# Split matmuls of a two-block transformer: first block sum of a weight tile formed as A22 plus A21 by a load and an adding DMA, and low parts of two tiles of the second FFN product by adding DMA

## The chip, the cores and the metric

The kernel runs on one core of one Trainium2 chip. The metric is the device time of one execution in microseconds (us). Before the change three runs took 1543.89, 1545.36 and 1546.64 us; the median is 1545.36 us.

## The reference

Two transformer blocks act on 256 latent tokens and 256 context tokens, with a model width of 1024. Each block has a feed-forward network (FFN), a mixer and a second FFN; the mixer of the first block is a gated short convolution, that of the second is attention with grouped keys. In the second block the context only feeds the attention, so the last FFN runs on the latent tokens alone. Every part sees a root-mean-square norm, a shift and a scale first and is added back through a gate:

```
def _modulate(t, g, shift, scale):
    return _rms(t, g) * (1 + scale) + shift
def _swiglu(h, w13, w2):
    gte, up = jnp.split(h @ w13, 2, axis=-1)
    return (jax.nn.silu(gte) * up) @ w2
lat = lat + 0.5 * mod[:, 0, 2] * _swiglu(_modulate(lat, norm_g[i, 0], mod[:, 0, 0], mod[:, 0, 1]), ffn_w13[i, 0], ffn_w2[i, 0])
```

FFN weights are 1024 x 5632 (`w13`) and 2816 x 1024 (`w2`), all in float32.

## The kernel before

**Split products.** TensorE (PE) gets each float32 operand as a high part (rounded to the type fp32r) and a low part (what is left), and one product is three matmuls: high x high (L136), low x high (L137), high x low (L138). ScalarE (ACT) copies a raw tile to its high part (L107, tiles `wh`), VectorE (DVE) subtracts to get the low part (L108, tiles `wl`); `split` does both. `split_far` (L111 to 114) does it without VectorE: ACT copies high (L112), ACT copies the negated high part into the low tile (L113), and a DMA issued by GpSimd (POOL) adds the raw weights from memory onto it (L114). Before the change only the block A22 of each weight tile goes this way (tiles `w4h`, `w4l`).

**Stages.** The FFNs with 512 tokens, (0,0), (0,1) and (1,0), run in thirds of 8, 7 and 7 column tiles of the 22. A third computes its column tiles of `h @ w13`, then `project` (L595) multiplies the gated result with the matching rows of `w2` for eight output tiles m = 0 to 7; `ws2` (L895) loads and splits the weights of output tile m. Tiles 0, 1 and 2 are asked for at the start of `project`, a further one whenever a tile is begun.

**Block products.** Most column tiles of `w13`, and those of the convolution's input product, are a `Pair` (L694): the weights of a tile are a 2 x 2 block matrix A11, A12, A21, A22, the activations a 2 x 2 block matrix B, and seven products of sums of blocks take the place of eight. The class `Blocks` holds the activation's blocks and their sums T1 to T4 (tiles `th`, `tl`); a `Pair` holds A11, A12, A22 and the sums S1 to S4. Its steps are `__init__` (loads, S1, and the splits of A11 and A12), `sums(0)` (S2 on VectorE, L732, and the split of the tile that holds S1 and S2), `sums(1)` (A22 by `split_far`, then S3 and S4 in one VectorE instruction, L740, and their split), and then the products on PE: `head` (A11, A12), `five` (S1), `six` (S2, S4), `seven` (S3), `four` (A22). In `__init__` SyncE (SP) loads r2 = [A22 | A12] (512 KB) and the right half of r1 = A11 (256 KB, L708); POOL writes -A22 into the left half of r1 (TENSOR_SCALAR, L710) and issues a DMA that adds A21 onto it (L713). So S1 = A21 - A22.

**Openings.** The convolution's product and the FFNs (0,1) and (1,0) begin with `opening` (L788): the last tiles of the stage before are still being finished while the norm of the first 256 tokens, then that of the other 256 tokens, is formed; two column tiles run without block products, half by half, and a `Pair` called `head` follows. `rms_sum` (L264) forms a norm: PE sums the squares (L269), ACT takes the root (L274), VectorE the reciprocal (L278), PE spreads it (L287), VectorE scales the activations (L299), and ACT and VectorE make the high and low parts (`bh` L391, `bl` L392, raw `hr` L396).

**Order of work.** A scheduler fixes the order of the instructions of each engine from the order of the code and from marks: what stands under `tc.issue_after(x)` comes behind the instruction x. Every engine then runs its list in order, and one that waits holds up all behind it. POOL's list holds L710, the adding DMAs L713 and L114, and the DMAs (L567) that add each gated result `yg` onto the residual `x`. Raw weights share 8 buffers (`wr`), the high and low tiles 4 each (`wh`, `wl`), A22's parts 2 each. L177 on VectorE are units of the modulation (scale, shift and gate of later stages) that fill gaps.

Of the kernel before, what the change touches and what calls it, by code (L numbers as in the profile page):

```python
# [9 lines left out]
F32 = mybir.dt.float32  # L10
# [3 lines left out]
ALU = mybir.AluOpType  # L14
AX = mybir.AxisListType

P = 128
# [3 lines left out]
T2 = 2 * S  # L21
# [27 lines left out]
def hybrid_kernel(ctx: ExitStack, tc: tile.TileContext, a: dict, out: bass.AP):  # L49
    nc = tc.nc  # L50
    const = ctx.enter_context(tc.tile_pool(name="const", bufs=1))
    wp = ctx.enter_context(tc.tile_pool(name="wp", bufs=2))
# [10 lines left out]
    def nm(s):  # L63
        uid[0] += 1
        return f"{s}{uid[0]}"
# [35 lines left out]
    def load_raw(src, n=1024):  # L101
        raw = wp.tile([P, 1024], F32, name=nm("wr"), tag="wr", bufs=8)
        nc.sync.dma_start(raw[:, :n], src)
        return raw

    def split(hi, lo, src):
        nc.scalar.activation(out=hi, in_=src, func=AF.Copy)  # L107
        return nc.vector.tensor_tensor(out=lo, in0=src, in1=hi.bitcast(F32), op=ALU.subtract)  # L108
# [139 lines left out]
        return get  # L248


    accs = {}

    def square_add(k, c0, c1):

# [9 lines left out]
    def rms_sum(s):  # L264

        pq = psmall("ss")
        for i in range(2):
            c = s * S + i * P
            nc.tensor.matmul(  # L269
                pq[:, S + i : S + i + 1], accs["t"][:, c : c + P], ones[:, 0:1],  # L270
                start=True, stop=True,
            )
        rs = tp.tile([P, 2], F32, name=nm("rs"), tag="rs")
        nc.scalar.activation(  # L274
            out=rs, in_=pq[:, S : S + 2], func=AF.Sqrt, scale=1.0 / D, bias=eps_t
        )
# [96 lines left out]
    class Blocks:  # L373
# [33 lines left out]
        def sums(self, n):  # L407

            r = self.raw
            b11, b12, b21, b22 = r[0, 0], r[0, 1], r[1, 0], r[1, 1]  # L410
            tt = nc.vector.tensor_tensor

            def keep(key, src):
                hi, lo = self.t[key] = hot("th"), hot("tl")
                split(hi, lo, src)

            if n == 0:
                tt(out=b11, in0=b12, in1=b11, op=ALU.subtract)
                keep("T1", b11)
            elif n == 1:  # L420
                tt(out=b12, in0=b22, in1=b12, op=ALU.add)
                tt(out=b22, in0=b22, in1=b11, op=ALU.add)
                keep("T2", b22)
            else:
                tt(out=b21, in0=b21, in1=b22, op=ALU.subtract)
                keep("T3", b12)
                keep("T4", b21)

    class FirstBlocks(Blocks):
# [13 lines left out]
        def sums(self):  # L443
            r = self.raw
            tt = nc.vector.tensor_tensor
            for key in ("T1", "T2", "T3", "T4"):
                self.t[key] = hot("th"), hot("tl")

            def keep(key, q, src):
                hi, lo = self.t[key]  # L450
                c = slice(q * T2, q * T2 + T2)
                split(hi[:, c], lo[:, c], src)

            b = lambda hf, s, q: r[2 * hf + q, s]
            for q in range(2):
                tt(out=b(0, 0, q), in0=b(0, 1, q), in1=b(0, 0, q), op=ALU.subtract)
                keep("T1", q, b(0, 0, q))
            for q in range(2):
                tt(out=b(0, 1, q), in0=b(1, 1, q), in1=b(0, 1, q), op=ALU.add)
                tt(out=b(1, 1, q), in0=b(1, 1, q), in1=b(0, 0, q), op=ALU.add)  # L460
# [236 lines left out]
    class Pair:  # L697
# [5 lines left out]

        def __init__(self, src, h):
            self.h, self.w, self.src = h, {}, src
            r2 = load_raw(src[:, 1024:2048])
            r1 = wp.tile([P, 1024], F32, name=nm("wr"), tag="wr", bufs=8)
            nc.sync.dma_start(r1[:, T2:], src[:, T2:1024])  # L708

            nc.gpsimd.tensor_scalar(  # L710
                out=r1[:, :T2], in0=r2[:, :T2], scalar1=-1.0, scalar2=None, op0=ALU.mult
            )
            nc.gpsimd.dma_start(out=r1[:, :T2], in_=src[:, :T2], accum_op=ALU.add)  # L713
            self.raw = [r1, r2]
            ts = half()
            for i, key in enumerate(("A11", "A12")):
                self.w[key] = [t[:, i * T2 : i * T2 + T2] for t in ts]
                split(*self.w[key], self.raw[i][:, T2:])

        def keep(self, keys, part):  # L720
            hi, lo = half()
# [4 lines left out]
        def sums(self, n):  # L726

            r1, r2 = self.raw
            s1, s2 = r1[:, :T2], r1[:, T2:]
            tt = nc.vector.tensor_tensor  # L730
            if n == 0:
                tt(out=s2, in0=s2, in1=s1, op=ALU.subtract)  # L732
                self.keep(("S1", "S2"), r1)
                return
            self.w["A22"] = [
                wp.tile([P, T2], F32R, name=nm(t), tag=t, bufs=2) for t in ("w4h", "w4l")
            ]
            split_far(*self.w["A22"], r2[:, :T2], self.src[:, 1024 : 1024 + T2])
            v = lambda t: t.rearrange("p (a c) -> p a c", a=2)
            tt(  # L740
                out=v(r2), in0=v(r2), in1=s2.unsqueeze(1).to_broadcast([P, 2, T2]),
                op=ALU.subtract,
            )
            self.keep(("S3", "S4"), r2)
# [44 lines left out]
    def opening(h, srcs, post):  # L789

        w = [load_w(srcs[0])]
        pp = [(psum("pg"), psum("pu")) for _ in range(2)]
        w13_mm(pp[0], w[0], h, range(KT), 0, S)
        flush(1)
        w.append(load_w(srcs[1]))
        at = w13_mm(pp[1], w[1], h, range(2), 0, S)
        with tc.issue_after(at):
            flush()
        with tc.issue_after(every[-1]):
            w13_mm(pp[1], w[1], h, range(2, KT), 0, S)  # L800
# [12 lines left out]

    def ffn(l, b, h, tot, gate, tail, gs=(), ev=(0, 0), z=None):
        gs = list(gs)
        i0 = 0
        for t, n in enumerate(THIRDS):
# [809 lines left out]
```

## Time and profile before

| | |
|---|---|
| median of 3 runs | 1545.36 us (1543.89 to 1546.64) |
| profiled execution | 1544.66 us |
| its span in the profile | 1542.9 us, so 1.8 us lie around it |
| PE busy | 1533.0 us, 99% |
| VectorE (DVE) busy | 1296.8 us, 84% |
| ACT busy | 850.5 us, 55% |
| POOL busy | 299.3 us, 19% |
| read from memory | 262.07 MB |

The profile shows one execution, with engine names as above; PEld is the weight load of a matmul, SP the queue of plain loads. A row of the timeline gives start and duration in us, engine, line, operation, output tile <- input tiles with their shape, and, in brackets, how long the engine was idle before and what ended that. Matmuls are pipelined: their durations overlap, and from start to start one with 256 columns takes 0.12 us and one with 512 columns 0.23 us. A larger distance from start to start is a stall of PE. A group of rows (`xN`) gives the total busy time and the mean in ns.

### The profile page before, as it was taken

How to read it: one execution, taken by the hardware profiler on the slowest of the kernel's cores; microseconds unless marked ns; L12 is line 12 of the kernel's file. 1: busy time of each engine (PE TensorE's matmuls, PEld its weight loads, DVE VectorE, ACT ScalarE, POOL GpSimd, SP SyncE). 2: the span in 40 equal slices, each digit the busy share in tenths (PEclk: the TensorE clock that was granted, in tenths of full speed). 3: DMA queues.
4: the chain of work that ended last, by engine and by line, in shares of the span. 5: the costliest groups of instructions: out<-in, count | busy, mean ns of one | idle time of the engine just before them, and what ended most of it. 6: DMA issues, size and time to landing. Idle time of an engine off the chain costs nothing.

```text
span 1542.9 us, 27460 instructions
## 1 busy us (share of the span) xinstructions
PE 1533.0 (99%) x10652; PEld 1424.7 (92%) x10652; DVE 1296.8 (84%) x1974; ACT 850.5 (55%) x1476; POOL 299.3 (19%) x265
## 2 busy tenths in 40 slices
PE   9999999999999999999999999999999999999999
PEld 7898998999999899989899899989999899998888
DVE  5889788898999999978979889958968788997676
ACT  5744554646665376446456476446456456774553
POOL 0003313402231012042142102142052002300000
PEclk9999999999999999999999999999999999999999
DMA  9568768775366645686796635786697743476562
GB/s 367 211 191 236 159 185 227 172 196 142 75 144 183 197 104 143 216 209 147 213 210 150 212 74 126 222 186 145 209 222 177 257 156 113 147 246 220 170 195 75
DMA packets 97474, 278.80 MB, mean 181 GB/s; under 512 B 11456, under 2 KB 13120, under 8 KB 97344
## 3 DMA queue, kind: packets, MB, share of 16 engines
q1 hardware_dynamic: 69408, 228.10, 45.8%
q0 software_dynamic: 25920, 47.20, 18.1%
q10 hardware_dynamic: 2016, 1.76, 0.4%
q8 instruction: 83, 1.36, 0.4%
q14 instruction: 47, 0.39, 0.1%
HBM read 262.07 MB, written 1.05 MB: 171 GB/s over the span
## 4 chain that ended last, share of the span: by engine, by line
PE 90%; DVE 5%; DMA 2%; issue 1%; ACT 1%; POOL 0%; SPq 0%; DVEq 0%; ACTq 0%; POOLq 0%
PE py L137 8%; PE py L136 8%; PE py L138 8%; PE p L138 8%; PE p L136 8%; PE p L137 8%; PE q L138 6%; PE q L136 6%; PE q L137 6%; PE py L144 2%; PE pu L144 2%; PE pg L144 2%; DMA wr<-in_w 2%; DVE wl L108 1%; PE py L146 1%
## 5 line engine op out<-in xcount | busy, mean ns | idle before, releaser
L107 ACT ACTIVATE wh<-wr 128x1024 fp32r<-128x1024 f32 (+2 forms) x454 | 401.3, 909 | 291.0 <-PE py L137 98.6
L108 DVE TENSOR_TENSOR wl<-wr,wh 128x1024 fp32r<-128x1024 f32 (+2 forms) x454 | 467.0, 1052 | 106.3 <-ACT wh L107 87.6
L177 DVE CUSTOM_DVE_ANT_0 junk<-wr,scbc,first 128x1024 bf16<-128x1024 f32 x209 | 271.0, 1296 | 2.3 <-DMA wr<-in_modT 0.3
L137 PE MATMUL py<-gl,wh 128*128 128x512 f32 (+1 forms) x570 | 213.4, 374 | 0.0
L136 PE MATMUL py<-gh,wh 128*128 128x512 f32 (+1 forms) x570 | 213.4, 374 | 0.0
L138 PE MATMUL py<-gh,wl 128*128 128x512 f32 (+1 forms) x570 | 212.8, 373 | 0.0
L710 POOL TENSOR_SCALAR wr<-wr 128x512 f32<-128x512 f32 x66 | 123.5, 1871 | 423.8 <-DMA wr<-in_w 223.0
L136 PE MATMUL p<-th,wh 128*128 128x256 f32 x528 | 149.5, 283 | 0.1
L138 PE MATMUL p<-th,wl 128*128 128x256 f32 x528 | 149.4, 283 | 0.0
L137 PE MATMUL p<-tl,wh 128*128 128x256 f32 x528 | 149.4, 283 | 0.0
L138 PEld LDWEIGHTS py<-gh,wl 128*128 128x128 f32 x570 | 107.3, 188 | 19.2
L136 PEld LDWEIGHTS py<-gh,wh 128*128 128x128 f32 x570 | 107.4, 188 | 18.3
L137 PEld LDWEIGHTS py<-gl,wh 128*128 128x128 f32 x570 | 107.4, 188 | 18.1
L138 PE MATMUL q<-bh,wl 128*128 128x256 f32 x400 | 113.2, 283 | 0.0
L136 PE MATMUL q<-bh,wh 128*128 128x256 f32 x400 | 113.2, 283 | 0.0
L137 PE MATMUL q<-bl,wh 128*128 128x256 f32 x400 | 113.2, 283 | 0.0
L136 PEld LDWEIGHTS p<-th,wh 128*128 128x128 f32 x528 | 101.3, 192 | 0.7 <-ACT sg L757 0.3
L137 PEld LDWEIGHTS p<-tl,wh 128*128 128x128 f32 x528 | 101.3, 192 | 0.4
L138 PEld LDWEIGHTS p<-th,wl 128*128 128x128 f32 x528 | 101.3, 192 | 0.0
L114 POOL DMA_DIRECT2D w4l<-in_w x56 | 53.5, 955 | 229.1 <-ACT w4l L113 182.7
L567 POOL DMA_DIRECT2D x<-yg x48 | 44.2, 985 | 212.6 <-ACT yg L564 180.5
L740 DVE TENSOR_TENSOR wr<-wr,wr 128x1024 f32<-128x1024 f32 x66 | 81.2, 1230 | 2.0 <-issue 0.3
(323 smaller groups left out, 4159.1 us busy)
## 6 DMA issues: line engine op xcount, KB each, us to landing
wr<-in_w SPq DMA_DIRECT2D x120, 512.0 KB, 4.8
wr<-in_modT SPq DMA_DIRECT2D x113, 512.0 KB, 4.9
wr<-in_w2b SPq DMA_DIRECT2D x64, 448.0 KB, 4.0
wr<-in_w2a SPq DMA_DIRECT2D x32, 512.0 KB, 4.6
wr<-in_w SPq DMA_DIRECT2D x56, 256.0 KB, 4.3
wr<-in_w POOLq DMA_DIRECT2D x56, 256.0 KB, 6.1
w4l<-in_w POOLq DMA_DIRECT2D x56, 256.0 KB, 6.1
x<-yg POOLq DMA_DIRECT2D x48, 256.0 KB, 7.3
```

The costliest lines, as they stand in the source:

```text
L107: nc.scalar.activation(out=hi, in_=src, func=AF.Copy)
L108: return nc.vector.tensor_tensor(out=lo, in0=src, in1=hi.bitcast(F32), op=ALU.subtract)
L114: nc.gpsimd.dma_start(out=lo, in_=src, accum_op=ALU.add)
L136: nc.tensor.matmul(ps, wh, mh, start=first, stop=False, **kw)
L137: nc.tensor.matmul(ps, wh, ml, start=False, stop=False, **kw)
L138: return nc.tensor.matmul(ps, wl, mh, start=False, stop=last, **kw).ins
L144: nc.tensor.matmul(ps, w[0], m[2], start=first and n == 0, stop=False)
L146: nc.tensor.matmul(ps[:, :S], w[1], m[0], start=False, stop=last and n == len(ms) - 1)
L177: nc.vector.tensor_tensor_reduce(out=junk, in0=raw, in1=scbc[:, v, :], scale=0.5 if ch in (2, 8) else 1.0, scalar=modb[:, l, col : col + 1 ...
L567: nc.gpsimd.dma_start(out=x[:, m, :], in_=t, accum_op=ALU.add)
L710: nc.gpsimd.tensor_scalar(out=r1[:, :T2], in0=r2[:, :T2], scalar1=-1.0, scalar2=None, op0=ALU.mult)
L740: tt(out=v(r2), in0=v(r2), in1=s2.unsqueeze(1).to_broadcast([P, 2, T2]), op=ALU.subtract,)
```

## The change

The change has three parts.

(A) `Pair.__init__` loads r1 = [A11 | A22] whole (512 KB) and first, POOL's DMA adds A21 onto its right half, and r2 = [A22 | A12] (512 KB) is loaded second. S1 is now A22 + A21. POOL's TENSOR_SCALAR is gone; A22 is loaded twice. The signs of S2 and of the activation's sums T follow, in as many instructions as before.

(B) `ws2` uses `split_far` for output tile m = 2 in all thirds and m = 3 in the first two thirds of the three FFNs with 512 tokens: 15 weight tiles of 512 KB (first third) or 448 KB.

(C) In `opening` the step `head.sums(1)` is marked to come behind the last root of a norm (L274) that has been written.

```
     def __init__(self, src, h):
-            r2 = load_raw(src[:, 1024:2048])
-            r1 = wp.tile([P, 1024], F32, name=nm("wr"), tag="wr", bufs=8)
-            nc.sync.dma_start(r1[:, T2:], src[:, T2:1024])
-            nc.gpsimd.tensor_scalar(
-                out=r1[:, :T2], in0=r2[:, :T2], scalar1=-1.0, scalar2=None, op0=ALU.mult
-            )
-            nc.gpsimd.dma_start(out=r1[:, :T2], in_=src[:, :T2], accum_op=ALU.add)
+            r1 = load_raw(src[:, T2 : T2 + 1024])
+            nc.gpsimd.dma_start(out=r1[:, T2:], in_=src[:, :T2], accum_op=ALU.add)
+            r2 = load_raw(src[:, 1024:2048])
...
-                split(*self.w[key], self.raw[i][:, T2:])
+                split(*self.w[key], self.raw[i][:, i * T2 : i * T2 + T2])
...
     def sums(self, n):
-            s1, s2 = r1[:, :T2], r1[:, T2:]
+            s1, s2 = r1[:, T2:], r1[:, :T2]
-                tt(out=s2, in0=s2, in1=s1, op=ALU.subtract)
-                self.keep(("S1", "S2"), r1)
+                tt(out=s2, in0=s1, in1=s2, op=ALU.subtract)
+                self.keep(("S2", "S1"), r1)
...
     def opening(h, srcs, post):
         head.head()
-        head.sums(1)
+        with tc.issue_after(roots[-1]):
+            head.sums(1)
         h.sums(2)
...
     def ws2(m):
-                split(hi[:, : n * P], lo[:, : n * P], raw[:, : n * P])
+                if tot == T2 and (m == 2 or m == 3 and t < 2):
+                    split_far(hi[:, : n * P], lo[:, : n * P], raw[:, : n * P], src[:, o : o + n * P])
+                else:
+                    split(hi[:, : n * P], lo[:, : n * P], raw[:, : n * P])
```

In the sums of the activations two additions become subtractions (`b12 = b22 - b12`, `b22 = b22 - b11`, in both classes), and `rms_sum` keeps its roots in a list `roots`. Behind `Pair.__init__` a line of the changed kernel has a lower number than the same line before, by 5 within the class: the adding DMA of S1 is L707 there (L713 before), the copies `sg<-p` of a `Pair` are L752 and L762 (L757 and L767 before), its silu is L768 (L773 before).

POOL, at the end of the second third of FFN (0,0), before. `wr` are raw weights, `w4l` is A22's low part, `yg` a gated result:

```order
L710 TENSOR_SCALAR wr_2272<-wr_2270 128x512
L713 DMA wr_2272<-in_w 128x512
L114 DMA w4l_2158<-in_w 128x512
L114 DMA w4l_2288<-in_w 128x512
L567 DMA x<-yg_2518 128x512
L567 DMA x<-yg_2537 128x512
L567 DMA x<-yg_2556 128x512
L567 DMA x<-yg_2600 128x512
L710 TENSOR_SCALAR wr_2747<-wr_2745 128x512
L713 DMA wr_2747<-in_w 128x512
```

The same place after:

```order
L707 DMA wr_2264<-in_w 128x512
L114 DMA w4l_2025<-in_w 128x512
L114 DMA w4l_2152<-in_w 128x512
L114 DMA w4l_2281<-in_w 128x512
L114 DMA wl_2406<-in_w2b 128x896
L114 DMA wl_2413<-in_w2b 128x896
L567 DMA x<-yg_2513 128x512
L567 DMA x<-yg_2532 128x512
L567 DMA x<-yg_2551 128x512
L567 DMA x<-yg_2595 128x512
L707 DMA wr_2740<-in_w 128x512
```

The TENSOR_SCALAR ahead of each adding DMA is gone, and the low parts of m = 2 and m = 3 (`wl` from `in_w2b`) stand ahead of the first additions onto `x`.

ACT, at the same place after, around the copies for m = 2 and m = 3 (`wh`, `wl`); before, the rows L113 are not there and the rows L112 are L107:

```order
L112 ACTIVATE wh_2405<-wr_2403 128x896
L762 COPY sg_2292<-p_2290 128x256
L113 ACTIVATE wl_2406<-wh_2405 128x896
L768 ACTIVATE sg_2292<-sg_2292 128x512
L107 ACTIVATE gh_2372<-gm_2201 128x512
L112 ACTIVATE wh_2412<-wr_2410 128x896
L113 ACTIVATE wl_2413<-wh_2412 128x896
```

Each negated copy has come in behind what already stood next to the high copy: for m = 2 it stands behind the copy of `p`, ahead of the silu.

VectorE in the opening of FFN (0,1), before. `bl` is the low part of a piece of the activations, `t` a scaled piece, `wl_6172` a low weight tile, `ri` the reciprocal for the second 256 tokens:

```order
L262 TENSOR_TENSOR acc_5727<-acc_5727,sq_6077 128x256
L299 SCALAR_TENSOR_TENSOR t_6080<-x,A_5974,ss_5990 128x256
L299 SCALAR_TENSOR_TENSOR t_6085<-x,A_5974,ss_5990 128x256
L392 SCALAR_TENSOR_TENSOR bl_6053<-t_6059,mod_6_3753,bh_6052 128x256
L108 TENSOR_TENSOR wl_6172<-wr_6167,wh_6171 128x1024
L392 SCALAR_TENSOR_TENSOR bl_6053<-t_6080,mod_6_3753,bh_6052 128x256
L392 SCALAR_TENSOR_TENSOR bl_6053<-t_6085,mod_6_3753,bh_6052 128x256
L278 RECIPROCAL ri_6163<-rs_6161 128x2
```

The same place after:

```order
L262 TENSOR_TENSOR acc_5706<-acc_5706,sq_6056 128x256
L299 SCALAR_TENSOR_TENSOR t_6059<-x,A_5953,ss_5969 128x256
L392 SCALAR_TENSOR_TENSOR bl_6032<-t_6038,mod_6_3742,bh_6031 128x256
L299 SCALAR_TENSOR_TENSOR t_6064<-x,A_5953,ss_5969 128x256
L392 SCALAR_TENSOR_TENSOR bl_6032<-t_6059,mod_6_3742,bh_6031 128x256
L278 RECIPROCAL ri_6142<-rs_6140 128x2
L108 TENSOR_TENSOR wl_6151<-wr_6146,wh_6150 128x1024
L392 SCALAR_TENSOR_TENSOR bl_6032<-t_6064,mod_6_3742,bh_6031 128x256
```

The low weight tile stands behind the third of the four `bl` and the reciprocal, no longer between the second and the third.

ACT at the same place after (`w4h_6407` is A22 of `head`, `w4h_6488` that of the next `Pair`); before, the two copies of `head` stood some twenty rows earlier, `w4h` of the next `Pair` some ten rows ahead of L274, and its `w4l` directly behind L274:

```order
L274 ACTIVATE rs_6140<-ss_6137,eps_t 128x2
L391 ACTIVATE bh_6031<-t_6064,mod_6_3742 128x256
L396 ACTIVATE hr_6030<-t_6064,mod_6_3742 128x256
L112 ACTIVATE w4h_6407<-wr_6306 128x512
L112 ACTIVATE w4h_6488<-wr_6475 128x512
L113 ACTIVATE w4l_6408<-w4h_6407 128x512
L396 ACTIVATE hr_6170<-t_6173,mod_6_3742 128x256
L113 ACTIVATE w4l_6489<-w4h_6488 128x512
```

All four copies of the two A22 have moved behind the root. On PE the order differs only in this opening.

More of the change, by code (lines that the diff above doesn't have):

```diff
@@ L248, in gate_of @@
         return get
-    accs = {}
+    accs, roots = {}, []
     def square_add(k, c0, c1):
@@ L273, in rms_sum @@
         rs = tp.tile([P, 2], F32, name=nm("rs"), tag="rs")
-        nc.scalar.activation(
+        roots.append(nc.scalar.activation(
             out=rs, in_=pq[:, S : S + 2], func=AF.Sqrt, scale=1.0 / D, bias=eps_t
-        )
+        ).ins)
         ri = tp.tile([P, 2], F32, name=nm("ri"), tag="ri")
@@ L420, in sums @@
             elif n == 1:
-                tt(out=b12, in0=b22, in1=b12, op=ALU.add)
-                tt(out=b22, in0=b22, in1=b11, op=ALU.add)
+                tt(out=b12, in0=b22, in1=b12, op=ALU.subtract)
+                tt(out=b22, in0=b22, in1=b11, op=ALU.subtract)
                 keep("T2", b22)
@@ L458, in sums @@
             for q in range(2):
-                tt(out=b(0, 1, q), in0=b(1, 1, q), in1=b(0, 1, q), op=ALU.add)
-                tt(out=b(1, 1, q), in0=b(1, 1, q), in1=b(0, 0, q), op=ALU.add)
+                tt(out=b(0, 1, q), in0=b(1, 1, q), in1=b(0, 1, q), op=ALU.subtract)
+                tt(out=b(1, 1, q), in0=b(1, 1, q), in1=b(0, 0, q), op=ALU.subtract)
                 keep("T2", q, b(1, 1, q))
@@ L705, in __init__ @@
             self.h, self.w, self.src = h, {}, src
+            r1 = load_raw(src[:, T2 : T2 + 1024])
+            nc.gpsimd.dma_start(out=r1[:, T2:], in_=src[:, :T2], accum_op=ALU.add)
             r2 = load_raw(src[:, 1024:2048])
-            r1 = wp.tile([P, 1024], F32, name=nm("wr"), tag="wr", bufs=8)
-            nc.sync.dma_start(r1[:, T2:], src[:, T2:1024])
-            nc.gpsimd.tensor_scalar(
-                out=r1[:, :T2], in0=r2[:, :T2], scalar1=-1.0, scalar2=None, op0=ALU.mult
-            )
-            nc.gpsimd.dma_start(out=r1[:, :T2], in_=src[:, :T2], accum_op=ALU.add)
             self.raw = [r1, r2]
```

## Prediction, made before the changed kernel was run

> **What bounds the kernel now.** I read the page first: the span, the busy shares and the chain of work that ended last.
>
> ```profile
> span 1542.9 us, 27460 instructions
> ...
> PE 1533.0 (99%) x10652; PEld 1424.7 (92%) x10652; DVE 1296.8 (84%) x1974; ACT 850.5 (55%) x1476; POOL 299.3 (19%) x265
> ...
> PE 90%; DVE 5%; DMA 2%; issue 1%; ACT 1%; POOL 0%; SPq 0%; DVEq 0%; ACTq 0%; POOLq 0%
> ```
>
> PE is busy for 99% of the span and holds 90% of the chain; no matmul is added or removed. Work taken from VectorE, ACT or POOL is worth only what PE stalls for it. So I read next where PE is not busy, in the table of windows (PE, PEld, DVE, ACT, POOL busy; clock; DMA share; GB/s). The change acts from about 50 us (the first `Pair`) to about 1240 us (the end of FFN (1,0)); these are the stretches up to 900 us, with the first FFN, the convolution and FFN (0,1).
>
> ```profile
> 50.00:353.00 303.00, 302.81 (x1967) 278.01 (x1966) 260.81 (x363) 155.21 (x260) 69.91 (x64) 1.00 0.72 190
> 353.00:545.00 192.00, 191.27 (x1413) 182.69 (x1412) 179.60 (x268) 107.60 (x181) 42.09 (x33) 1.00 0.55 147
> 545.00:900.00 355.00, 353.38 (x2504) 333.28 (x2503) 305.97 (x436) 198.43 (x345) 86.27 (x79) 1.00 0.68 176
> ```
>
> PE idles 0.19 + 0.73 + 1.62 = 2.5 us in 850 us, at a granted clock of 1.00. A modelled matmul outlasts its start-to-start distance (0.28 against 0.12 us), so a short stall can hide in a busy row; I therefore measure stalls from start to start. By either measure there are only a few us to win here, and any amount to lose. The last rows read were those around each stall.
>
> **Part A, what it removes.** POOL's negation goes, and one load grows.
>
> ```profile
> L710 POOL TENSOR_SCALAR wr<-wr 128x512 f32<-128x512 f32 x66 | 123.5, 1871 | 423.8 <-DMA wr<-in_w 223.0 <-DVE acc L262 46.6 <-DVE wl L108 44.5
> ```
>
> 66 x 1.87 = 123.5 us of POOL go. L732, which forms S2, waits for S1's adding DMA; I found one place where this reaches PE, ahead of the last third of FFN (0,0):
>
> ```profile
> 254.50 1.78 POOL L710 TENSOR_SCALAR wr<-wr 128x512 f32<-128x512 f32 x1 [4.54 <-DMA wr<-in_w]
> 256.69 0.92 POOL L713 DMA_DIRECT2D wr<-in_w  x1 [0.41 <-POOL wr L710]
> ...
> 262.66 0.69 DVE L732 TENSOR_TENSOR wr<-wr 128x512 f32<-128x512 f32 x1 [1.72 <-DMA wr<-in_w]
> ...
> 266.81 3.37 DVE L108 TENSOR_TENSOR wl<-wr,wh 128x1024 fp32r<-128x1024 f32 x3
> ...
> 267.73 0.28 PE L137 MATMUL q<-tl,wh 128*128 128x256 f32 x1
> 268.09 0.39 PE L138 MATMUL q<-th,wl 128*128 128x256 f32 x1
> ...
> 269.27 0.28 PE L138 MATMUL q<-th,wl 128*128 128x256 f32 x1
> 269.66 0.39 PE L136 MATMUL p<-th,wh 128*128 128x256 f32 x1
> ...
> 269.22 0.39 ACT L757 COPY sg<-p 128x256 f32<-128x256 f32 x1
> ```
>
> The load lands at about 254.5, POOL negates for 1.78 us, issues the addition at 256.69, and S2 starts when that has landed, at 262.66. The first low part of S1 is taken up from there, and PE gets it at 268.09, 0.36 us after the matmul before instead of 0.12: a stall of **0.24 us**. At 269.66 PE stands again, 0.39 - 0.12 = **0.27 us**; the copy of `p` that must be out before the next product writes there ended at 269.61, late because ACT was held up in the same chain. After the change the addition can be issued when the first load has landed, 256.69 - 254.50 = 2.2 us earlier. Nothing else on POOL's list has come in between, and S2 needs r1 alone. Next in line, the second low part, has over 2 us as well, so I take both stalls as gone: **-0.5 us**. Bounds: 0, if the load that now comes first lands 2 us later for its place in the queue, and -0.5.
>
> The negation also slows VectorE beside it. In the convolution:
>
> ```profile
> 428.07 1.11 DVE L732 TENSOR_TENSOR wr<-wr 128x512 f32<-128x512 f32 x1
> ...
> 430.85 1.21 DVE L108 TENSOR_TENSOR wl<-wr,wh 128x1024 fp32r<-128x1024 f32 x1
> ...
> 428.04 1.48 POOL L710 TENSOR_SCALAR wr<-wr 128x512 f32<-128x512 f32 x1 [5.99 <-DVE wl L108]
> ...
> 431.71 0.28 PE L137 MATMUL p<-tl,wh 128*128 128x256 f32 x1
> 432.11 0.39 PE L138 MATMUL q<-th,wl 128*128 128x256 f32 x1
> ```
>
> L732 takes 1.11 us beside L710, against 0.69 at 262.66. Everything behind it is 0.42 us late, and PE waits 0.40 - 0.12 = **0.28 us** for the low part that ends at 432.06. Without L710 it would be there at 431.64, and PE wants it at 431.83: **-0.28 us**.
>
> On this row a rule of the Trainium skill bears. SBUF — State Buffer, section Who interferes with whom, says that a VectorE instruction with two inputs in SBUF contends with a GpSimd instruction that reads SBUF, over a port pair held exclusively, so that the later one is blocked for the whole of the earlier. The row shows the contention and not its size: L732 began 0.03 us after L710 and lost 0.42 us, not the 1.45 us until L710's end. By the rule more VectorE time would come free; the 0.28 us on PE stay what they are, since a stall can't give back more than it lost.
>
> The price of A is traffic: 66 x 256 KB = 17.3 MB more in plain loads.
>
> ```profile
> DMA packets 97474, 278.80 MB, mean 181 GB/s; under 512 B 11456, under 2 KB 13120, under 8 KB 97344
> ...
> q1 hardware_dynamic: 69408, 228.10, 45.8%
> q0 software_dynamic: 25920, 47.20, 18.1%
> ...
> wr<-in_w SPq DMA_DIRECT2D x120, 512.0 KB, 4.8
> ...
> wr<-in_w SPq DMA_DIRECT2D x56, 256.0 KB, 4.3
> wr<-in_w POOLq DMA_DIRECT2D x56, 256.0 KB, 6.1
> ...
> x<-yg POOLq DMA_DIRECT2D x48, 256.0 KB, 7.3
> ```
>
> A 512 KB load lands 0.5 us later than a 256 KB one (4.8 against 4.3). With B's 7.3 MB the traffic is some 303 MB against 278.8; at each queue's present share for its bytes, 17.3 x 45.8 / 228.1 + 7.3 x 18.1 / 47.2, that is 6% more, from 64% to 70%. The stretch from 50 to 353 us lost only 0.19 us at 72%, so I cost it at nothing; that stretch itself goes to about 79%, and what covers it is the eight raw buffers, through which a load is issued ahead of its use. If the cover is gone, loads are late everywhere and the second rival below holds.
>
> **Part B.** 15 subtractions leave VectorE (about 17 us at 1.1 to 1.2 us each), as many negated copies come to ACT and 15 adding DMAs to POOL. VectorE's gain is worth nothing by itself, since no stall seen in those stretches ends on such a subtraction. ACT's copy stands where ACT idles; POOL's issue (0.9 us) only holds up the additions onto `x`. What counts is the time at which the low part is there:
>
> ```profile
> 220.91 0.95 ACT L107 ACTIVATE wh<-wr 128x896 fp32r<-128x896 f32 x1 [0.49 <-PE p L137]
> 221.77 0.35 ACT L767 COPY sg<-p 128x256 f32<-128x256 f32 x1
> 223.86 0.63 ACT L773 ACTIVATE sg<-sg 128x512 f32<-128x512 f32 x1 [1.74 <-DVE sg L769]
> ...
> 228.65 0.95 ACT L107 ACTIVATE wh<-wr 128x896 fp32r<-128x896 f32 x1 [2.35 <-PE p L137]
> ...
> 233.90 0.39 PE L138 MATMUL py<-gh,wl 128*128 128x512 f32 x1
> ...
> 241.39 0.39 PE L138 MATMUL py<-gh,wl 128*128 128x512 f32 x1
> ```
>
> For m = 2 of the second third the high part ends at 221.86, the copy of `p` at 222.12, the negated copy (0.95) at 223.07, inside the 1.74 us gap ahead of the silu. PE's first matmul with the low part starts at 233.90: **10.8 us** are left for issue and landing. For m = 3: 229.60 + 0.95 = 230.55, and PE at 241.39, again 10.8 us. No row has an addition of 448 KB. From below it is the plain load's time; from above the 7.3 us of the additions onto `x` scaled by the bytes, 7.3 x 1.75 = 12.8 us. I take 7.1 us: a packet of q0 costs 18.1% x 16 x 1542.9 / 25920 = 172 ns, 192 KB more are 6 more packets of 2 KB on each of 16 engines, so 1.0 us on top of the 6.1 us of the rows from `in_w`, which are the same kind of transfer. That leaves over 3 us: **0**.
>
> DMA: Bandwidth & Descriptors, section Anatomy of one DMA — SWDGE (gpsimd) path, in the Trainium skill, fits such a DMA as 2 us plus bytes at 436 GB/s: 3.1 us for 448 KB. By that there is more room still; the 6.1 us of the 256 KB rows, against 2.6 by the fit, speak against taking it.
>
> **Part C** acts in the three openings. In those of the convolution and FFN (1,0) VectorE's order stays, and ACT's four copies of A22 move into a gap behind the root. In FFN (0,1) the order of VectorE and PE moves too:
>
> ```profile
> 547.46 1.06 ACT L107 ACTIVATE wh<-wr 128x1024 fp32r<-128x1024 f32 x1 [2.23 <-PE py L137]
> ...
> 558.73 1.31 ACT L396 ACTIVATE hr<-t,mod 128x256 f32<-128x256 f32 x3 [2.32 <-DVE t L299]
> ...
> 548.97 0.39 PE L136 MATMUL pg<-bh,wh 128*128 128x256 f32 x1 [1.43 <-ACT bh L391]
> ...
> 556.12 0.39 PE L137 MATMUL pg<-bl,wh 128*128 128x256 f32 x1 [0.20 <-DVE bl L392]
> ...
> 554.46 1.22 DVE L108 TENSOR_TENSOR wl<-wr,wh 128x1024 fp32r<-128x1024 f32 x1
> 555.59 1.23 DVE L392 SCALAR_TENSOR_TENSOR bl<-t,mod,bh 128x256 fp32r<-128x256 f32 x2
> ```
>
> The 1.43 us stall at 548.97 is ACT's: it stood for a buffer (2.23 us), copied a weight tile, and only then the first `bh`. These rows keep their order: it stays. The stall at 556.12 waits for a `bl` that stood behind the weight tile's subtraction (554.46, 1.22 us). That `bl` is now ahead of it, 1.1 us sooner: **-0.36 us** (0.20 shown idle and the 0.16 by which a row outlasts its distance). What could be late next is the reciprocal's result, ahead of the fourth `bl` on PE's list; the root no longer stands behind the last pieces on ACT, and I find it in time by over 1 us. The four copies, at most 0.63 us each as the instruction of this shape at 223.86, are 2.5 us; ACT waited 2.32 us for `t` at 558.73, and comes to that place 0.6 us sooner since a copy ahead of it is gone. Bounds: -0.36, and +0.4 if the new order only exchanges that stall for one of its kind.
>
> **Sum.** -0.24 - 0.27 - 0.28 - 0.36 = -1.15 us. The profiled execution's 1544.66 becomes 1543.5; it lay 0.7 us below the median of the runs shown, so for the median I say **1544.2 us**. A difference under 0.2%, 3.1 us, is about what a measurement of this kernel can't tell from none.
>
> **The rivals.**
> *Slower: the adding DMAs of B land late.* The place is PE's first high x low matmul of m = 2 and m = 3 (L138), in `project`. For it speaks that additions onto `x` take 7.3 us for half the bytes, and that they follow directly behind; against it the 6.1 us of the other rows. It decides from 10.8 us. At 12.8 us each of nine tiles of 448 KB costs 2.0 us, 18 us in all, without the larger tiles of the first third: **1562 us**; at 11.8 us it is 9 us, 1553.
> *Slower: loads late by traffic.* If the added 24 MB make the full windows fuller, more of the 66 first loads are late as the one at 254.50 was. That one cost PE the 0.5 us above; ten more like it give **1549 us**. Against it: 65 others cost nothing at the load of before.
> *Faster: the stall at 548.97 goes as well*, and the rest of the 2.5 us of idle time with it, because ACT has fewer copies to make around the openings. Against it: ACT idled for 2.23 us ahead of it, for a buffer that PE holds. 1544.2 - 2.3 is **1542 us**, just beyond 0.2%.
> *The change does nothing for PE*: the stalls come back where the next operand is late. **1545.4 us**.
>
> **How the numbers follow.** Chances: forecast 0.45, nothing for PE 0.17 (both within 0.2%), faster 0.16, loads late 0.09, adding DMAs late 0.13. Of the faster case three quarters lie beyond 1542.3, of the loads' two thirds beyond 1548.4: faster 0.12, same 0.69, slower 0.19. The range reaches from 1540.5, the faster case less half of the 2.75 us by which the runs of before differ, to 1549.5, past the late loads and short of most of the late adding DMAs; the bounds of the sum for A and C (-1.15 to +0.1 us) lie within it.
>
> **What would show it.** Right: no TENSOR_SCALAR ahead of the additions on POOL, S2 at 262.66 about 2 us sooner, VectorE below 1280 us busy, no stall at 268, 432 and 556, that at 549 still there. Wrong: idle time of PE that ends on a DMA at L138, issue-to-landing times of the 448 KB additions near 11 us, or L732 and L107 waiting longer for loads than before.

## The result: 0.2% faster, and not for the reason that carried most of the forecast

The changed kernel took 1542.58 us (median of 15 runs, 1541.88 to 1543.74), the kernel before beside it 1545.40 us (15 runs, 1543.89 to 1548.86): a ratio of 0.9978, interval 0.9971 to 0.9985. That is 2.8 us less, where 1.15 us less was forecast; the time lies inside the stated range, 1.6 us below the forecast. The profiled executions differ by 2.3 us (1544.66 and 1542.35).

The page of the changed kernel, its first lines and its chain:

```profile
span 1540.5 us, 27351 instructions
...
PE 1530.6 (99%) x10652; PEld 1423.3 (92%) x10652; DVE 1267.0 (82%) x1959; ACT 864.4 (56%) x1491; POOL 194.3 (13%) x214
...
PE 95%; DVE 2%; DMA 1%; ACT 0%; issue 0%; SPq 0%; POOL 0%; DVEq 0%; ACTq 0%; POOLq 0%
```

VectorE lost 29.8 us: the 17 us of the subtractions, and some 13 us of slowdown beside POOL's TENSOR_SCALAR (part A alone, below, takes 14 us off VectorE). POOL lost 105 us; ACT gained 14. PE's own share of the chain went from 90% to 95%. In the list of what PE waited for between 45 and 1238 us two waits are left:

```profile
PE pg L136 <- ACT bh L391: 1.4, 1, 1.4
PE p L138 <- DVE wl L108: 0.6, 1, 0.6
```

The first is the stall at 549 us, which the forecast left in place, now at 547.65; the second is one at 409, also of before. The stalls at 268, 432, 556 and 929 are gone. Ahead of the last third of FFN (0,0) the rows on POOL, VectorE and PE now read:

```profile
253.14 0.88 POOL L707 DMA_DIRECT2D wr<-in_w  x1 [3.28 <-DMA wr<-in_w]
...
261.04 0.69 DVE L727 TENSOR_TENSOR wr<-wr 128x512 f32<-128x512 f32 x1 [1.92 <-DMA wr<-in_w]
...
262.91 3.21 DVE L108 TENSOR_TENSOR wl<-wr,wh 128x1024 fp32r<-128x1024 f32 x3
...
267.50 0.28 PE L137 MATMUL q<-tl,wh 128*128 128x256 f32 x1
267.62 0.28 PE L138 MATMUL q<-th,wl 128*128 128x256 f32 x1
```

The addition onto S1 is issued at 253.14 and not at 256.69, S2 starts at 261.04 and not at 262.66, and PE passes from 267.50 to 267.62 without a stall. In the opening of FFN (0,1) VectorE's reciprocal and the last `bl` stand as the order had shown, and only the long stall ahead is left:

```profile
553.30 0.17 DVE L278 RECIPROCAL ri<-rs 128x2 f32<-128x2 f32 x1
553.38 1.21 DVE L108 TENSOR_TENSOR wl<-wr,wh 128x1024 fp32r<-128x1024 f32 x1
554.50 0.48 DVE L392 SCALAR_TENSOR_TENSOR bl<-t,mod,bh 128x256 fp32r<-128x256 f32 x1
...
547.65 0.39 PE L136 MATMUL pg<-bh,wh 128*128 128x256 f32 x1 [1.43 <-ACT bh L391]
```

The lines on the queues and the landing times of the changed kernel (KB each, median us to landing):

```profile
q1 hardware_dynamic: 69408, 245.40, 49.0%
q0 software_dynamic: 28080, 54.47, 21.0%
...
wr<-in_w SPq DMA_DIRECT2D x176, 512.0 KB, 5.1
...
wl<-in_w2b POOLq DMA_DIRECT2D x9, 448.0 KB, 8.9
wl<-in_w2a POOLq DMA_DIRECT2D x6, 512.0 KB, 9.2
```

Traffic grew to the 70% that was worked out. The new adding DMAs take 8.9 and 9.2 us, not 7.1. The fit of the Trainium skill (DMA: Bandwidth & Descriptors, section Anatomy of one DMA — SWDGE (gpsimd) path) gives an estimate of 3.1 us for 448 KB; the measurement is nearly three times that.

One more thing is seen in the runs: those of before spread over 5 us, those of the changed kernel over 1.9 us. So the profile said that the stalls of the forecast went, but not which part took them, nor why the median moved by more than the profiled executions. The experiments take the parts one by one.

### The profile page after: what moved, and what is told of

The parts are those of the page before. It is cut to its first block, busy times and chain, and to the rows that moved or that the text cites. A ratio compares the mean times of both kernels' runs of the same rounds, so it can differ in the third digit from the quotient of the medians.

```text
span 1540.5 us, 27351 instructions
## 1 busy us (share of the span) xinstructions
PE 1530.6 (99%) x10652; PEld 1423.3 (92%) x10652; DVE 1267.0 (82%) x1959; ACT 864.4 (56%) x1491; POOL 194.3 (13%) x214
## 3 DMA queue, kind: packets, MB, share of 16 engines
q0 software_dynamic: 28080, 54.47, 21.0%
## 4 chain that ended last, share of the span: by engine, by line
PE 95%; DVE 2%; DMA 1%; ACT 0%; issue 0%; SPq 0%; POOL 0%; DVEq 0%; ACTq 0%; POOLq 0%
PE py L137 9%; PE py L136 9%; PE py L138 9%; PE p L138 8%; PE p L137 8%; PE p L136 8%; PE q L138 6%; PE q L136 6%; PE q L137 6%; PE py L144 2%; PE pu L144 2%; PE pg L144 2%; PE pg L136 1%; PE pg L138 1%; PE py L146 1%; PE pu L136 1%
## 5 line engine op out<-in xcount | busy, mean ns | idle before, releaser
L108 DVE TENSOR_TENSOR wl<-wr,wh 128x1024 fp32r<-128x1024 f32 (+2 forms) x439 | 443.5, 1033 | 129.1 <-ACT wh L107 110.7
L107 ACT ACTIVATE wh<-wr 128x1024 fp32r<-128x1024 f32 (+2 forms) x439 | 386.4, 906 | 256.2 <-PE py L137 99.3
L177 DVE CUSTOM_DVE_ANT_0 junk<-wr,scbc,first 128x1024 bf16<-128x1024 f32 x209 | 267.4, 1279 | 3.6 <-DMA wr<-in_modT 1.4
L138 PE MATMUL py<-gh,wl 128*128 128x512 f32 (+1 forms) x570 | 212.8, 373 | 0.0
L138 PE MATMUL p<-th,wl 128*128 128x256 f32 x528 | 149.4, 283 | 0.0
L138 PEld LDWEIGHTS py<-gh,wl 128*128 128x128 f32 x570 | 107.3, 188 | 19.1
L138 PE MATMUL q<-bh,wl 128*128 128x256 f32 x400 | 113.2, 283 | 0.0
L707 POOL DMA_DIRECT2D wr<-in_w x56 | 49.0, 875 | 452.1 <-DMA wr<-in_w 127.4
L138 PEld LDWEIGHTS p<-th,wl 128*128 128x128 f32 x528 | 101.3, 192 | 0.0
L573 DVE SCALAR_TENSOR_TENSOR x<-py,mod,x 128x256 f32<-128x256 f32 x117 | 52.8, 478 | 33.2 <-PE py L138 22.2
```

The source lines that it names most:

```text
L138: return nc.tensor.matmul(ps, wl, mh, start=False, stop=last, **kw).ins
L177: nc.vector.tensor_tensor_reduce(out=junk, in0=raw, in1=scbc[:, v, :], scale=0.5 if ch in (2, 8) else 1.0, scalar=modb[:, l, col : col + 1 ...
L573: nc.vector.scalar_tensor_tensor(out=x[:, m, s * S : s * S + S], in0=ps[:, o : o + S], scalar=g[:, m, s : s + 1], in1=x[:, m, s * S : s * ...
L707: nc.gpsimd.dma_start(out=r1[:, T2:], in_=src[:, :T2], accum_op=ALU.add)
```

## The experiments

Each was timed beside runs of the kernel before on the same chip: the parts alone and the last version on one chip, where the kernel before took 1545.95 us by the median, the others on a second, where it took 1545.26 us. Ratios are to these. Before the first four ran, the theory was the forecast's with the stalls of the traces: part A, by the shorter chain to S1 and by relieving VectorE, ends most stalls, part C those of the second opening, B none. The rival: VectorE's relief in B is what helps.

**Part A alone** (the changed kernel without these):

```
-        with tc.issue_after(roots[-1]):
-            head.sums(1)
+        head.sums(1)
-                if tot == T2 and (m == 2 or m == 3 and t < 2):
-                    split_far(...)
-                else:
-                    split(...)
+                split(hi[:, : n * P], lo[:, : n * P], raw[:, : n * P])
```

> Part A alone on the kernel before (first block sums as A22 + A21, without the low parts by adding DMA and without the mark in the openings). Theory (late S1 chain and VectorE slowed by POOL's TENSOR_SCALAR): the stalls at 268, 432 and 929 us of the trace of before are gone, those of the second opening (556 us) stay; the span is 1.5 us shorter, and the runs, which before scatter up to 1548.9 us, scatter less. Rival (VectorE's relief in part B or the new order of part C gives the gain): within 0.5 us of before, same scatter.

Measured: 1546.99 us, ratio 1.0009 (1.0001 to 1.0018): not faster, and by the interval slightly slower; the runs spread as widely as before (1545.1 to 1550.5). The profiled execution is the slowest of them. ACT and PE in the opening of the convolution, PE at the place of S1, and the window of 3.4 us behind the stall at 375, with the columns of the earlier table of windows:

```profile
366.96 0.63 ACT L112 ACTIVATE w4h<-wr 128x512 fp32r<-128x512 f32 x1 [3.08 <-DMA wr<-in_cw_b]
...
375.10 0.61 PE L269 MATMUL ss<-ones,acc 128*128 128x1 f32 x4 [1.51 <-DVE acc L262]
...
270.32 0.38 PE L138 MATMUL q<-th,wl 128*128 128x256 f32 x1 [1.63 <-DVE wl L108]
...
376.30:379.70 3.40, 3.40 (x17) 3.40 (x17) 1.92 (x5) 1.75 (x3) 0.89 (x1) 0.50 0.47 76
```

The stall at 268 has grown to 2.3 us. A new one of 3.4 us (from start to start, with what follows it) stands at 375, another of 2.2 us at 898. Of the 3.4 us, 1.7 are the wait and some 1.5 the clock: behind the wait the granted clock was 0.50 for 3.4 us, and matmuls with 256 columns came 0.21 us apart and not 0.12. The cause of both waits: ACT waits 3.08 us for the load of A22, which part A has made the second, and behind that copy on ACT's list stand the squares of the norm, for which PE's sum waits.

**Part B alone** (the `ws2` lines of the diff on the kernel before).

> Part B alone on the kernel before (low parts of m = 2 and m = 3 by adding DMA). Theory: within 0.3 us of before, same scatter, since no stall ends on those subtractions; all stalls of before stay. Rival 1 (17 us less VectorE work is what helps): 1 us or more faster. Rival 2 (the adding DMAs cost something that part A hides): 1 us or more slower, with PE idle at L138 in the second product.

Measured: 1544.60 us, 0.9990 (0.9981 to 0.9999), with a narrow spread (1543.7 to 1545.4). The stall at 268 is gone, those at 556 and 929 stay. The rival has it: 1.35 us below the kernel before, where the theory allowed 0.3 us and no stall gone.

**Part C alone** (the mark on the kernel before).

> Part C alone on the kernel before (the mark in the openings). Theory: the short stalls of the second opening at 556 us go, span 0.8 us shorter, all others stay, scatter as before. Rival (the order alone does nothing without A and B): within 0.2 us of before.

Measured: 1545.15 us, 0.9994 (0.9984 to 1.0003): inside the bounds of no change. The stalls at 556 are gone, that at 268 is there (1.4 us), and one of 0.6 us at 605 is new: there VectorE now runs L740 (602.75) ahead of the low part that PE waits for (603.89), where before the low part (602.26) stood ahead of L740 (603.40).

The first theory fell: A alone loses, and B ends the stall for which A had been credited. The new one: A's reordered load harms the openings unless C moves ACT's copy of A22 behind the norm, and B brings the loads at 268 forward. The pairs test it.

**A and B without C**

> Parts A and B, without the mark of part C. New theory: part A loads A22 second, and without part C ACT's copy of A22 stands ahead of the norm's squares in the openings of the convolution and FFN (1,0), so the stalls of 3.4 us at 375 and 2.2 us at 898 that part A alone showed stay, while B ends that at 270: 4 to 6 us slower than the whole change, some 1547 us. Rival 1 (effects add up: A alone +1.0, B alone -1.3): 1545.6 us. Rival 2 (B's earlier loads bring A22 in time as well): within 1 us of the whole change, 1543.5 us.

Measured: 1546.52 us, 1.0000 (0.9991 to 1.0009). ACT and PE in the opening of FFN (1,0):

```profile
891.32 0.63 ACT L112 ACTIVATE w4h<-wr 128x512 fp32r<-128x512 f32 x1 [3.02 <-DMA wr<-in_w]
...
895.86 0.61 PE L269 MATMUL ss<-ones,acc 128*128 128x1 f32 x4 [1.84 <-DVE acc L262]
```

3.6 us are lost there, 2.0 of them the wait and some 1.3 a granted clock of 0.50 for 3.4 us behind it, and 0.7 us at 374; none at 268. This profile too is of the slowest of the eleven runs, and another stretch at half clock lies at 23 us, ahead of all that the change touches. Rival 1's 1545.6 lies 0.9 below the median and inside the interval; the stalls decide for the theory.

**A and C without B**

> Parts A and C, without the low parts by adding DMA. New theory (C ends the wait for A22 in the openings, B is what brings the loads ahead of the last third of FFN (0,0) sooner): no stall at 375 and 898, a stall of 1 to 2.5 us at 268 to 270 stays, about 1544.5 us. Rival of the prediction (A itself ends the stall at 268): within 0.3 us of the whole change.

Measured: 1544.55 us, 0.9992 (0.9983 to 1.0001): 1.9 us are lost at 269, nothing beyond the 0.4 us of before at 372 and 892. POOL, VectorE and PE at S1, with the shorter chain:

```profile
256.23 0.89 POOL L707 DMA_DIRECT2D wr<-in_w  x1 [5.77 <-DMA wr<-in_w]
...
263.63 0.69 DVE L727 TENSOR_TENSOR wr<-wr 128x512 f32<-128x512 f32 x1 [3.25 <-DMA wr<-in_w]
...
269.06 0.39 PE L138 MATMUL q<-th,wl 128*128 128x256 f32 x1 [1.28 <-DVE wl L108]
```

There is no negation ahead of the addition, yet it is issued only 0.5 us sooner than in the kernel before (256.69), because the `Pair`'s first load lets POOL go on at 256.23 and not at 254.50, though SP's last load of `w2` went out no later (243.55). S2 starts 7.4 us behind that issue, where it was 6.0, and so 1.0 us later than before (262.66). The later load and the longer addition eat the 2.2 us that the missing negation saves.

**B and C without A**

> Parts B and C, with the first block sum as before. New theory (A by itself only ends VectorE's slowdown beside POOL's TENSOR_SCALAR): stalls at 268, 432 and 556 gone, 0.5 us at 929 to 934 there; 0.5 us slower than the whole change, about 1543.3 us. Rival (A carries 1.5 us, as the prediction's sum and the stalls have it): 1544 us or more.

Measured: 1544.05 us, 0.9988 (0.9980 to 0.9997). None at 268, 432 and 556; 0.5 us at 928 to 932, as expected, and 0.6 us at 603, which was not. The time is the rival's (1544 us or more): by the medians A is worth 1.5 us on top of B and C (0.9988 to 0.9978; the intervals overlap), three times what the theory said. The stalls that are here and not with A add up to 1.1 us, and the one at 268 is not among them.

**Why B ends the stall at 268: buffers or VectorE's time.** B alone, with VectorE kept as busy:

```
                     split_far(hi[:, : n * P], lo[:, : n * P], raw[:, : n * P], src[:, o : o + n * P])
+                    h32 = hi[:, : n * P].bitcast(F32)
+                    nc.vector.tensor_tensor(out=spare[:, : n * P], in0=h32, in1=h32, op=ALU.subtract)
```

> Part B alone, and for each of its 15 tiles VectorE subtracts the high part from itself into a spare tile (same shape, not used by anything), so that VectorE is as busy as before while raw buffers are still freed by ACT and the low parts still come by DMA. Theory VT (B helps because VectorE gets to the modulation units sooner, whose raw buffers the loads wait for): the stall at 268 is back, 0.5 us or more, time as before the change. Theory RB (B helps because the raw buffers of m = 2 and m = 3 come free with ACT's copy): no stall at 268, as with B alone.

Measured: 1546.11 us, 1.0000 (0.9991 to 1.0009); the stall is back. The rows that tell it apart are SP's issue of the last load of `w2` ahead of the `Pair`s, POOL's wait for a `Pair`'s load, and the window from 218 to 245 us. In the kernel before, with what SP's loads waited for:

```profile
243.77 0.33 SPq L103 DMA_DIRECT2D wr<-in_w2b  x1
...
218.00:245.00 27.00, 27.00 (x154) 23.80 (x154) 26.16 (x41) 10.22 (x17) 2.67 (x3) 1.00 0.76 239
...
SPq L103 <- DVE mod L177: 23.0, 9, 5.6
```

With B alone:

```profile
241.79 0.33 SPq L103 DMA_DIRECT2D wr<-in_w2b  x1
...
252.84 1.48 POOL L710 TENSOR_SCALAR wr<-wr 128x512 f32<-128x512 f32 x1 [2.31 <-DMA wr<-in_w]
...
218.00:245.00 27.00, 27.00 (x154) 23.79 (x154) 26.25 (x44) 11.99 (x19) 4.40 (x5) 1.00 0.96 289
```

With B and VectorE kept busy (its lines have numbers 2 higher), with PE's row at the stall:

```profile
244.02 0.33 SPq L105 DMA_DIRECT2D wr<-in_w2b  x1
...
256.28 1.90 POOL L712 TENSOR_SCALAR wr<-wr 128x512 f32<-128x512 f32 x1 [5.69 <-DMA wr<-in_w]
...
270.14 0.38 PE L140 MATMUL q<-th,wl 128*128 128x256 f32 x1 [1.88 <-DVE wl L110]
```

VectorE is busy for 26.2 of these 27 us. SP's loads wait mostly for its modulation units (23.0 us in nine waits between 205 and 262 us in the kernel before), because a unit's raw weights hold one of the eight buffers until VectorE has read them. Without two subtractions VectorE is 2 us further, the load of `w2` goes out at 241.79 in place of 243.77, and the `Pair`'s load lands by 252.84 in place of 254.50. With VectorE kept busy it goes out at 244.02, the `Pair`'s load lands at 256.28, and PE loses 2.5 us. The other differences of B (buffers freed by ACT, low parts by DMA) are still there, so they don't carry the gain.

**What A itself gives.** The changed kernel, and POOL negates A22 into a spare tile behind each addition:

```
             r2 = load_raw(src[:, 1024:2048])
+            nc.gpsimd.tensor_scalar(
+                out=spare, in0=r2[:, :T2], scalar1=-1.0, scalar2=None, op0=ALU.mult
+            )
```

> The whole change, and behind each adding DMA of a first block sum POOL negates A22 into a spare tile that nothing reads, 66 times as before. Theory (what A itself gives is that POOL's TENSOR_SCALAR no longer slows VectorE): stalls of 0.3 to 0.6 us come back at about 929 and 605, some 1 us slower than the whole change, VectorE's L108 again at 1235 ns or more. Rival (A gives the shorter chain to S1 alone): as the whole change, 1542.6 us, no such stalls.

Measured: 1544.58 us, 0.9996 (0.9987 to 1.0005), against 0.9978 without it. The group of the added instruction, and VectorE, POOL and PE in the convolution (L110 and L140 are L108 and L138 of the change):

```profile
L711 POOL TENSOR_SCALAR spare<-wr 128x512 f32<-128x512 f32 x66 | 118.3, 1792 | 106.8 <-DMA wr<-in_w 90.5 <-DMA wr<-in_cw_b 10.1 <-DMA wr<-in_cw_cx 6.3
...
430.13 1.63 DVE L110 TENSOR_TENSOR wl<-wr,wh 128x1024 fp32r<-128x1024 f32 x1
...
429.77 1.80 POOL L711 TENSOR_SCALAR spare<-wr 128x512 f32<-128x512 f32 x1 [1.14 <-DMA wr<-in_cw_cx]
...
431.03 0.28 PE L139 MATMUL p<-tl,wh 128*128 128x256 f32 x1
431.82 0.39 PE L140 MATMUL q<-th,wl 128*128 128x256 f32 x1 [0.52 <-DVE wl L110]
```

A stall of 0.8 us with its restart is back at 431.82, behind a subtraction that took 1.63 us in place of 1.22; 0.4 us are back at 933, also behind VectorE. The place that was expected at 605 stayed clear. VectorE is busy for 1282.2 us in place of 1267.0, and its L108 with 1024 columns takes 1240 ns by the mean in place of 1220, as expected. So 1.3 us by the spans and 2.0 us by the medians are TENSOR_SCALAR's absence, though the place where it hurts moves with the timing. What POOL's own list loses by the added instruction is not separated from this.

**The order of the loads.** A and B without C, with r2 loaded first:

```
+            r2 = load_raw(src[:, 1024:2048])
             r1 = load_raw(src[:, T2 : T2 + 1024])
             nc.gpsimd.dma_start(out=r1[:, T2:], in_=src[:, :T2], accum_op=ALU.add)
-            r2 = load_raw(src[:, 1024:2048])
```

> Parts A and B without the mark of part C, and with A22's tile r2 loaded first again, r1 second. Theory (parts A and B without C were slow because ACT's copy of A22 stands ahead of the norm and waits for a load that has become the second): the stalls of 0.7 to 3.6 us at about 373 and 896 fall to the 0.4 us of before, 2 to 3 us faster than A and B without C, some 1543.7 us. Rival (the added traffic makes the loads late in the openings): those stalls stay, 1546.5 us.

Measured: 1546.57 us, 1.0009 (1.0000 to 1.0018): no gain. The stall at 895 is back to 0.4 us, that at 373 is not (0.8 us), where ACT still waits for an A22, and S1, now behind the second load, is late elsewhere (1.5 us at 104, 0.4 us at 271), with 0.6 us more at 546 and 0.5 us at 793:

```profile
365.78 0.63 ACT L112 ACTIVATE w4h<-wr 128x512 fp32r<-128x512 f32 x1 [2.54 <-DMA wr<-in_cw_cx]
...
104.47 0.39 PE L138 MATMUL q<-th,wl 128*128 128x256 f32 x1 [1.29 <-DVE wl L108]
```

The theory holds for one of the two places. How much of the other is the order of the loads and how much the larger traffic stays open. That r1 comes first is needed for S1, and C is then needed for A22.

**The deadline of the adding DMAs.** The changed kernel with `m in (1, 2)` for `m == 2`:

> The whole change, with the low part of m = 1 by adding DMA too, in all thirds of the three FFNs: nine tiles whose first use by PE comes some 7.7 us after ACT's negated copy. Theory (an adding DMA of 448 or 512 KB takes the 9 us from issue to landing that the changed kernel's trace shows): PE stalls at L138 by 1 to 2 us at each of the nine, 9 to 18 us slower than the whole change. Rival (a landing of 7.1 us, as predicted): below 3 us slower.

Measured: 1564.67 us, 1.0125 (1.0111 to 1.0139). What PE waits for in the whole trace, and POOL and PE in the second third of FFN (0,0), with the landing of the nine and six tiles of 448 KB:

```profile
PE py L138 <- DMA wl<-in_w2b: 13.0, 6, 3.3
PE py L138 <- DMA wl<-in_w2a: 4.7, 3, 2.0
...
224.21 0.86 POOL L114 DMA_DIRECT2D wl<-in_w2b  x1 [5.54 <-ACT sg L762]
...
231.20 0.40 PE L137 MATMUL py<-gl,wh 128*128 128x512 f32 x1
234.90 0.50 PE L138 MATMUL py<-gh,wl 128*128 128x512 f32 x1 [3.30 <-DMA wl<-in_w2b]
...
wl<-in_w2b POOLq DMA_DIRECT2D x15, 448.0 KB, 10.0
```

PE stalls at nine places, one for each tile, by 1.1 to 5.1 us from start to start, 25 us in the profiled execution, the slowest of the four. Idle time is 17.7 us of that (13.0 and 4.7 in the list), 2.0 us per tile. Behind the three longest waits the granted clock was 0.50 for 3.4 us each, which makes up most of the rest. By the medians the loss is 22 us, beyond the 18 us expected. 10.7 us pass from the issue of that addition to PE's restart. This is the first rival's mechanism, and its price per tile; for m = 2 and m = 3 the changed kernel escapes it, by the median landing of 8.9 us, with under 2 us to spare.

**A better version tried.** The changed kernel, in which the second half of the second column tile of an opening is split behind the activations' first parts (`late` only puts that split aside until it is called):

```
-        w.append(load_w(srcs[1]))
+        w.append(load_w(srcs[1], late=True))
...
             flush()
+        with tc.issue_after(bhs[-7]):
+            rest.pop()()
```

> The changed kernel with one more mark: in the openings the split of the second half of the second column tile is issued behind the first parts of the activations, so that ACT does not stand for a weight buffer ahead of them. Theory (the 1.6 us stall at 548 us is ACT's order): that stall falls by 1.0 us or so, span about 1539.5 us. Rival (the activations' t is what is late, or the delayed weight tile stalls PE instead): span within 0.3 us of 1540.5 or longer.

Measured: 1542.27 us, 0.9978 (0.9970 to 0.9987), so no difference from the change that can be told; the span is 1540.9 us, where about 1539.5 had been expected, so the rival (1540.5 or longer) has it. ACT and PE in the opening:

```profile
546.32 0.91 ACT L396 ACTIVATE bh<-t,mod 128x256 fp32r<-128x256 f32 x2 [2.18 <-DVE t L304]
...
546.88 0.38 PE L141 MATMUL pg<-bh,wh 128*128 128x256 f32 x1 [0.43 <-ACT bh L396]
```

The stall falls from 1.43 to 0.43 us of idle time, and ACT now waits for `t`; from start to start the stall shrinks by 0.9 us, of which some 0.4 are lost again in short stalls at 553 and 555.

The stalls of the profiled executions in us, from start to start beyond the usual distance, restarts included (0.4 us at 372 and 896 are there in every kernel; the 3.4 and the 3.6 hold 1.3 to 1.5 us of half clock; "-" is none):

| | 268 | 372 | 432 | 556 | 605 | 896 | 929 to 934 | median, ratio |
|---|---|---|---|---|---|---|---|---|
| before | 0.7 | 0.4 | 0.4 | 0.6 | - | 0.4 | 0.5 | |
| A | 2.3 | 3.4 | - | 0.4 | - | 2.2 | - | 1.0009 |
| B | - | 0.4 | - | 0.6 | - | 0.4 | 0.5 | 0.9990 |
| C | 1.4 | 0.4 | - | - | 0.6 | 0.4 | 0.5 | 0.9994 |
| A, B | - | 0.7 | - | 0.4 | - | 3.6 | - | 1.0000 |
| A, C | 1.9 | 0.4 | - | - | - | 0.4 | - | 0.9992 |
| B, C | - | 0.4 | - | - | 0.6 | 0.4 | 0.5 | 0.9988 |
| A, B, C | - | 0.4 | - | - | - | 0.4 | - | 0.9978 |

## Why the prediction was right in sign and range, and wrong in two steps

- **What bounds the kernel:** right. What the change won in the profile are stalls of PE that together were 2 to 3 us.
- **A, -0.5 us at 268:** the stall went, but not by this step. It stays, at 1.4 to 2.5 us, in A, in C, in A with C, and in B with VectorE kept busy; with B it is gone whether S1's chain is shorter or not, but for 0.4 us where r2 is loaded first. Two steps failed. One is the 2.2 us: the forecast's own bound of 0, a first load that lands 2 us later, is what A with C shows (1.7 us later, and the addition 1.4 us longer). Traffic had been charged at nothing, and at this place the transfers take longer though they are issued as early. The other is the sentence on part B, "VectorE's gain is worth nothing by itself, since no stall seen in those stretches ends on such a subtraction": the stall came some 25 us later, by way of modulation units, raw buffers and loads.
- **A, -0.28 us at 432:** the mechanism was right, as the added TENSOR_SCALAR showed, the place was chance: with B or C alone the stall at 432 is gone although the TENSOR_SCALAR is there. Its absence is worth 1.3 to 2.0 us over all places, among them that near 930, which the forecast had not found. The stall at 605 goes with A as well, but did not come back with the added TENSOR_SCALAR; what ends it stays open. The rule of the Trainium skill (SBUF — State Buffer, section Who interferes with whom) was again borne out in kind and not in size: VectorE lost 0.41 us beside an instruction of 1.80. The page calls the shared pair an exclusive lock; the full block it words for VectorE's two-port modes, and of an instruction with two inputs in SBUF it says that it contends.
- **A's price:** nothing had been charged but traffic, and that costs little once B and C are there. What was missed is that A22's load became the second, and ACT's list puts its copy ahead of a norm: 5.6 us in the profile of A alone, some 1.5 of them the clock. Part C was read as a gain of 0.36 us in one opening; its main work is to prevent this in the two others.
- **C, -0.36 us:** 0.6 us; the restarts were not counted (below). In C alone and in B with C the new order exchanges it for 0.6 us at 605, which the forecast had as its bound; only with A is the gain kept.
- **B, landing 7.1 us:** mis-sized, 8.9 to 9.2; the margin of 10.8 us was right, and so no stall came of it. That a larger addition has more packets was wrong: q0 carried 25920 packets for 180 additions of 256 KB and now carries 28080 for 195, so 144 each, whatever the size. The packets became longer, not more.
- **The median** moved by 0.5 us more than the profiled executions. The stall at 268 was 0.7 us in the profile of before and 1.4 to 2.5 us in the other profiles that have it, and of the kernels timed in 11 or 15 runs those without it and without a late A22 spread by 0.8 to 2.8 us, those with either by 2.8 to 5.9. That it is this stall that varies from run to run is argued from that, not shown. The clock goes with it in the record: of the 87 runs of the kernel before beside the experiments, 12 have a mean granted clock of 0.998 or 0.999, and they took 1547.0 to 1551.4 us, among the longest; with A and B it is 7 runs of 11, with the whole change 1 of 15, its slowest.

## What to carry to other kernels

Where an engine is off the critical path but frees the buffers that loads wait for, its time is worth something far from where it is saved: ask the load queue's waits, not only PE's. When two loads change places, look up every instruction that waits for the one that is now second, on in-order engines above all, and what stands behind it. And take parts of a change one by one: here A alone, C alone, and A with B gave nothing or a loss, and A brings a gain only beside the other two.

## What the runs showed that was not expected

A stall of PE costs more than its wait. In the kernel before, the matmul behind the stalled one also comes late, 0.22 us after it in place of 0.12:

```profile
268.09 0.39 PE L138 MATMUL q<-th,wl 128*128 128x256 f32 x1
268.31 0.28 PE L136 MATMUL q<-th,wh 128*128 128x256 f32 x1
268.43 0.28 PE L137 MATMUL q<-tl,wh 128*128 128x256 f32 x1
```

The same 0.10 us follow the other stalls looked at (432, 556, 929), so five short stalls cost half a microsecond more than their waits. A longer stall can cost more still: behind waits, from start to start, of 1.7 us (A alone, 375), 2.0 us (A with B, 896) and 2.8 to 3.5 us (three places with m = 1) the granted clock was 0.50 for 3.4 us. An estimate from that is up to 1.7 us each, half of the 3.4. Behind others of 1.8 to 2.0 us (A alone, 270 and 898) it stayed at 1.00; what decides is open. And an adding DMA of 448 KB took 8.9 us by the median, against 6.3 us for one of 256 KB in the same execution: 2.6 us for 192 KB more, where the time of the packets had given 1.0.
